# One more weight slot, one more raw tile, a longer lead of the first block, and later modulation sums in a two-layer decoder trunk

## The chip, the core and the metric

The kernel runs on one core of a Trainium2 chip. The metric is the device time of one execution in microseconds. TensorE (PE) does the matmuls, VectorE (DVE) and ScalarE (ACT) the elementwise work, GpSimd (POOL) a few small operations and some loads; SyncE (SP) issues nearly all loads from HBM.

## The reference, cut to what matters

256 tokens of width 1024 go through two layers. Each layer has three sub-layers, each with a residual:

```
mod = silu(c) @ ada_w[l] + ada_b[l]            # 9 vectors of 1024: shift, scale, gate of 3 sub-layers
h = rms_norm(x)*(1+sc1) + sh1;  x += 0.5*g1*swiglu(h)       # w_in 1024x5632, w_out 2816x1024
h = rms_norm(x)*(1+sc2) + sh2;  x += g2*token_mix(h)        # w_in 1024x2884, w_out 1024x1024
h = rms_norm(x)*(1+sc3) + sh3;  x += 0.5*g3*swiglu(h)
out = rms_norm(x)                                            # after the last layer
```

`token_mix` is a causal gating of 128-token chunks beside attention over the 64 best keys of an indexer. All is float32. The modulation vectors cost one pass over 75 MB of `ada_w`; all weights together are about 250 MB.

## The kernel before, in words

**Split products.** A float32 product is made of three fast ones: each weight tile is split into a high part `whi` (ACT, L455) and a low part `wlo` (DVE, L456), as the activations are, and `mm3` (L489 to L491) adds high by high, high by low, low by high. A *unit* is one weight tile of 128x1024. A split of a unit is called a conversion below.

**Phases and blocks.** The six sub-layers are phases 0 to 5: f, m, f, f, m, f (f for the feed-forward, m for the mixing). The tokens are two blocks of 128, b0 and b1. A generator per block (`ffn_gen`, `mix_gen`, `project`) yields after each unit. An f phase has 66 units: 8 for each block by itself, 36 that take both blocks at once (`joint_gen`, 256 columns, L672 to L676), then the 22 of the output product (`project`). An m phase has 24 units and 8 of `project`.

**Order.** `both` advances b0 while it is at most `LAG` items ahead of b1, else b1: so b0 runs `LAG`+1 units ahead, and at the end of a phase b1 has that many units left by itself. Then the next phase begins with b0 alone. After each item `item_done` runs what was deferred by a count of items, and `pump` issues up to one conversion.

**Slots.** Converted weights live in `NB` slots. `ring` keeps the order: a conversion may be issued when the slot `NB` conversions back has been released, and b1's item releases it. So in a steady stretch one conversion follows each item of b1, and its ACT part waits until TensorE has ended that item. Raw loads have `NRAW` tiles.

**Ends of a phase.** `project` goes through its units with both halves of 512 columns per unit, except the last `TAIL` units: there the first half of the columns is finished over all `TAIL` units, then the second. After the first half DVE makes `update` (L539, L541), ACT the squares (L502); after the second half `update` again, then `after_sub`: the sum (L510), the power on POOL (L512), the scaling (L516) and, `TRL` = 5 items later, `tr`: TensorE transposes of the scaled block (L733), scale and shift out of PSUM (ACT L527, DVE L529), and the split (ACT L534, DVE L535). `hold` keeps `pump` still for the item in which `after_sub` runs and the next one, and, for b1, also after the first half.

**Modulation.** `weave` puts the 8 tiles of each modulation vector between the units of a phase, evenly from unit `F0` to `F1` (f phases; `FA0`, `FA1` in phase 0) or `MA0` to `MA1` (m phases). `pump` adds such a tile to the sum when it comes to it in the sequence: the first by ACT (L435), the other seven by DVE (L440), one 128x1024 operation each. Eight items after the last tile a shift or scale vector is summed over partitions by two sets of four transposes and reductions (L403), a gate vector by four matmuls with ones. `VA1` to `VB2` say how many vectors each phase takes: 5, 1, 4 in layer 0, then 5, 0 and the last one.

In an m phase `sgu_out` (L954, hook of unit 22 of b0) writes `u`, which TensorE transposes one unit later.

Of the kernel before, what the change touches and what calls it, by code (L numbers as in the profile page):

```python
# [20 lines left out]
KF = DFF // P  # L21
DEPTH = 2
EPS = 1e-6
NB = 10
LEADJ = 8
LAG = 6
NRAW = 7
HOLD = 3
TAIL = 3
VX = 188  # L30
ADA_D = 8
D_EVP = 0
# [4 lines left out]
D_SC = 12  # L37
EV_D = 1
TR_D = 3
MA0 = 8  # L40
MA1 = 30
NG = 4
GW = D // NG
# [11 lines left out]
VA1 = 5  # L55
VA2 = 1
VA3 = 4
VB1 = 5
VB2 = 0
F0 = 14  # L60
F1 = 62
ADA0_ACT = 1
COL_D = 2
YH = 1
# [33 lines left out]
def trunk(ctx, tc, x_in, c_in, pos_in, ada_w, ada_b, norm_ffn1, ffn1_w_in, ffn1_w_out,  # L98
          norm_mix, mix_w_in, sgu_w, sgu_b, mix_w_out, norm_ffn2, ffn2_w_in, ffn2_w_out,
          final_norm, out):  # L100
    nc = tc.nc
# [3 lines left out]
    small = ctx.enter_context(tc.tile_pool(name="small", bufs=2))  # L105
    rawp = ctx.enter_context(tc.tile_pool(name="rawp", bufs=NRAW))
    hlp = ctx.enter_context(tc.tile_pool(name="hlp", bufs=NB))
    aap = ctx.enter_context(tc.tile_pool(name="aap", bufs=2))
# [4 lines left out]
    def take():  # L113
        return banks.pop(0)

    def give(*ts):
        banks.extend(ts)
# [134 lines left out]
    def weave(us, ads, lo, hi):  # L252
        res, n = [], len(ads)
        tot = max(n // KD * (KD + GAP), 1)
        pos = [lo + (hi - lo) * (i // KD * (KD + GAP) + i % KD + GAP // 2) // tot for i in range(n)]
        ai = 0
        for i, e in enumerate(us):
            while ai < n and pos[ai] <= i:
                res.append(ads[ai])
                ai += 1  # L260
            res.append(e)
        res += ads[ai:]
        return res
# [11 lines left out]
    names = [(l, nm) for l in range(DEPTH) for nm in ("A1", "B1", "G1", "A2", "B2", "G2", "A3", "B3", "G3")][2:]  # L275
    cuts = [VA1, VA2, VA3, VB1, VB2, len(names)]
    for l in range(DEPTH):
# [6 lines left out]
        for q in range(3):  # L284
            vl.append(sum((vecs(a, [nm]) for a, nm in names[:cuts[3 * l + q]]), []))
            names = names[cuts[3 * l + q]:]
        w1 = weave(u1, vl[0], FA0 if l == 0 else F0, FA1 if l == 0 else F1)
        if l == 0:
# [9 lines left out]
        seq += w1  # L298
        seq += weave(u2, vl[1], MA0, MA1)
        seq += weave(u3, vl[2], F0, F1)  # L300
    hold = [0]
# [8 lines left out]
    def defer(n, fn):  # L310
        pend.append([n, fn])
# [15 lines left out]
    def dma_fill():  # L327
        while dp[0] < len(seq):
# [5 lines left out]
            else:  # L334
                if n_r[0] - n_rd[0] >= NRAW:
                    break
# [75 lines left out]
    def pump(quota=2, force=False):  # L412
# [3 lines left out]
        while sp[0] < len(seq) and quota > 0:  # L416
# [8 lines left out]
            if e["k"] == "w" and not force and len(W) - wcur[0] >= lead[0]:  # L425
                break
            if need and r >= NB and not ring[r - NB]:
                assert not force, (r, ring[r - NB:], wcur, [q[0] for q in pend])
                break
# [36 lines left out]
    wcur = [0, 0]  # L466
    lead = [NB]

    def next_w(b):
        while wcur[b] >= len(W):  # L470
            pump(1, force=True)
        e = W[wcur[b]]
        wcur[b] += 1
        kt, cols = e["kt"], e["cols"]
        n = kt * cols
        return (e["hi"][:, :n].rearrange("p (k c) -> p k c", k=kt),
                e["lo"][:, :n].rearrange("p (k c) -> p k c", k=kt), e["slot"])

    def release(b, w):
        if b == 1:  # L480
            ring[w[2]] = True
# [6 lines left out]
    def mm3(ps, ahi, alo, whi, wlo, first, last):  # L488
        T.matmul(ps, ahi, whi, start=first, stop=False)  # L489
        T.matmul(ps, ahi, wlo, start=False, stop=False)  # L490
        T.matmul(ps, alo, whi, start=False, stop=last)  # L491
# [6 lines left out]
    def square(b, sl, first):  # L498
        if first:
            ssq[b] = [small.tile([P, 4], F32, name="ss", tag="ss"), 0]  # L500
        ss, c = ssq[b]
        S.activation(xm[b][:, sl], x[b][:, sl], AF.Square, accum_out=ss[:, c:c + 1])  # L502
        ssq[b][1] += 1
        if ssq[b][1] == 3:
            V.tensor_tensor(ss[:, 0:1], ss[:, 0:1], ss[:, 1:2], op=ALU.add)
# [32 lines left out]
    def update(b, l, i, acc, sl):  # L538
        V.scalar_tensor_tensor(xm[b][:, sl], acc, 1.0 if i == 2 else 0.5, vec[(l, "G", i)][:, sl],  # L539
                               op0=ALU.mult, op1=ALU.mult)  # L540
        V.tensor_tensor(x[b][:, sl], x[b][:, sl], xm[b][:, sl], op=ALU.add)  # L541

    def final_scale(b, sl):
        V.scalar_tensor_tensor(x[b][:, sl], x[b][:, sl], D ** 0.5, fin_g[0][:, sl], op0=ALU.mult, op1=ALU.mult)
# [25 lines left out]
    def project(b, pi, n, operand, hook):  # L570
        _, l, i, _ = phases[pi]
        final = pi + 1 == len(phases)
        parts = PARTS if final and b == 1 else HALF
        bk = [take() for _ in parts]
        acc = [t[:, :sl.stop - sl.start] for t, sl in zip(bk, parts)]

        def part(k, w, h):
            ahi, alo = operand(k)
            mm3(acc[h], ahi, alo, w[0][:, 0, parts[h]], w[1][:, 0, parts[h]], k == 0, k == n - 1)
        for k in range(n - TAIL):  # L580
            w = next_w(b)
            release(b, w)
            for h in range(len(parts)):
                part(k, w, h)
            hook(k)
            yield
        ws = [next_w(b) for _ in range(TAIL)]
        for h, sl in enumerate(parts):
            for i_ in range(TAIL):
                part(n - TAIL + i_, ws[i_], h)  # L590
                if h + 1 == len(parts):
                    release(b, ws[i_])
                if i_ == 1 and h == 0:
                    hook(n - TAIL)
                    yield
            if h < 2:
                hook(n - TAIL + h + 1)
            update(b, l, i, acc[h], sl)
            give(bk[h])
            if h == 0 and SQ_D and not final:  # L600
                defer(SQ_D, lambda b=b, sl=sl: square(b, sl, True))
            else:
                square(b, sl, h == 0)
            if final and h + 1 == len(parts):
                final_scale(b, parts[0])
            if h + 1 == len(parts):
                after_sub(b, pi)
            elif b == 1:
                hold[0] = 1 << 20
            if h != 1 or len(parts) == 2:  # L610
                yield
# [557 lines left out]
    for pi, (kind, l, i, n) in enumerate(phases):  # L1169
        with ExitStack() as es:  # L1170
            env = {}
            cnt = [0, 0]
            gens = {}

            def item(b):
                if b not in gens:
                    gens[b] = (ffn_gen if kind == "f" else mix_gen)(b, pi, env)
                next(gens[b])
                cnt[b] += 1
                item_done()  # L1180
                hold[0] -= 1
                if pi == 0 and cnt[0] > 10:
                    next(rope_it, None)
                pump(PQ)

            if pi == 0:
                with tc.tile_pool(name="startp", bufs=NSRAW) as sp_:
                    startp[0] = sp_
                    start(item)
            env["pool"] = es.enter_context(tc.tile_pool(name=f"ph{pi}", bufs=2))  # L1190
            one = es.enter_context(tc.tile_pool(name=f"po{pi}", bufs=1))
            if kind == "f":
                env["aThi"] = one.tile([P, KF, 2, P], F32R, name="aThi")
                env["aTlo"] = one.tile([P, KF, 2, P], F32R, name="aTlo")
            else:
                env["kiT"] = one.tile([P, 2 * P], F32, name="kiT")
                env["kT"] = one.tile([P, 4, 2 * P], F32, name="kT")
                env["v"] = one.tile([P, 2, 512], F32, name="vS")
            def both(stop):
                while cnt[1] < stop:  # L1200
                    if cnt[0] < stop and cnt[0] - cnt[1] <= LAG:
                        item(0)
                        if pi == len(phases) - 1 and cnt[0] == n - 10:
                            fin_g[0] = vecp.tile([P, D], F32, name="vec", tag="vec")
                            nc.sync.dma_start(fin_g[0], bcast_row(final_norm, D))
                    else:
                        item(1)
            if kind == "f":
                both(n - KF)
                lead[0] = LEADJ  # L1210
                for q, _ in enumerate(joint_gen(env)):
                    item_done()
                    hold[0] -= 1
                    if pi == 0:
                        next(rope_it, None)
                        next(rope_it, None)
                    pump(2)
                    if i == 1 and q == 4:
                        sgu_prep(l, env)
                        sguT[l] = env["sgu_T"]  # L1220
                        defer(6, env["sgu_fin"])
                lead[0] = NB
            both(n)


# [27 lines left out]
```

## Time and profile before

| | before |
|---|---|
| median of three runs | 1020.39 us (1020.06 to 1020.56) |
| the profiled execution | 1017.07 us |
| its span, first to last instruction | 1015.3 us |
| TensorE busy in it | 983.5 us, 97% |
| VectorE busy | 775.9 us, 76% |
| ScalarE busy | 539.0 us, 53% |
| GpSimd busy | 19.8 us, 2% |
| HBM read | 251.27 MB, 249 GB/s over the span |
| mean granted clock of TensorE | 0.997 |

The span is what the trace covers; 1.8 us of the execution lie around it. A busy share is over the whole span. Matmuls overlap one another in the records and their ends are modelled, so the distance from one matmul's start to the next says how fast TensorE goes. "Idle before" in a row is the time in which the engine stood still before that instruction, with what ended it.

### The profile page before, as it was taken

The page shows a single profiled execution, that of the slowest core. Times are in us where ns is not written, and L with a number is a line of the kernel's source. Part 1 is how long each engine was busy: PE and PEld are TensorE (multiplying, and loading weights), DVE is VectorE, ACT ScalarE, POOL GpSimd, SP SyncE. Part 2 cuts the span into 40 slices and gives each one's busy share as a digit, 9 for nine tenths or more (in the row PEclk, how much of TensorE's full clock was granted, in tenths as well). Part 3 has the DMA queues.
Part 4 walks back from the last instruction along what each step waited for, and adds up shares of the span by engine and source line. Part 5 has one row for each costly group of instructions (what it writes and reads, how often), then busy time and mean ns, then how long its engine had stood idle before and what let it go on. Part 6 is the DMA issues. An engine that isn't in the chain of part 4 may idle for free.

```text
span 1015.3 us, 16506 instructions
## 1 busy us (share of the span) xinstructions
PE 983.5 (97%) x6352; PEld 871.8 (86%) x6352; DVE 775.9 (76%) x1095; ACT 539.0 (53%) x832; POOL 19.8 (2%) x39
## 2 busy tenths in 40 slices
PE   5999999998999999999999999999999999999997
PEld 3699998887778799998878999987778879999886
DVE  3898988877997888887679798885879787566554
ACT  5575454446576645543456555534667766445341
POOL 4000000000000000000000000000000000000000
PEclk9999999999999999999999999999999999999999
DMA  9989899867664598878758899896555547665631
GB/s 328 340 309 339 316 380 346 317 203 230 192 188 146 168 346 313 313 273 289 273 161 289 341 330 353 320 343 193 157 147 156 154 146 259 250 218 188 217 116 42
DMA packets 109775, 253.40 MB, mean 250 GB/s; under 512 B 8499, under 2 KB 26981, under 8 KB 109697
## 3 DMA queue, kind: packets, MB, share of 16 engines
q1 hardware_dynamic: 108864, 251.20, 71.9%
q8 instruction: 50, 0.82, 0.3%
q0 software_dynamic: 544, 0.63, 0.2%
q10 hardware_dynamic: 288, 0.52, 0.1%
q14 instruction: 29, 0.23, 0.1%
HBM read 251.27 MB, written 1.05 MB: 249 GB/s over the span
## 4 chain that ended last, share of the span: by engine, by line
PE 84%; DVE 9%; ACT 3%; issue 2%; POOL 1%; DMA 1%; SPq 0%; POOLq 0%; ACTq 0%; DVEq 0%
PE bank L489 13%; PE bank L672 13%; PE bank L674 13%; PE bank L676 13%; PE bank L491 13%; PE bank L490 13%; PE bank L733 3%; DVE wlo L456 2%; DVE x L541 1%; ACT whi L455 1%; DVE xm L539 1%; PE bank L1047 1%; POOL rstd L512 1%; DVE aacc L1053 1%; DMA x<-in_x_dram 1%
## 5 line engine op out<-in xcount | busy, mean ns | idle before, releaser
L456 DVE TENSOR_TENSOR wlo<-raw,whi 128x1024 fp32r<-128x1024 f32 (+1 forms) x328 | 392.4, 1212 | 111.7 <-ACT whi L455 110.9
L455 ACT ACTIVATE whi<-raw 128x1024 fp32r<-128x1024 f32 (+1 forms) x328 | 334.4, 1045 | 217.4 <-PE bank L491 136.3
L672 PE MATMUL bank<-hThi,whi 128*128 128x256 f32 x1152 | 321.0, 279 | 0.0
L674 PE MATMUL bank<-hTlo,whi 128*128 128x256 f32 x1152 | 319.6, 277 | 0.0
L676 PE MATMUL bank<-hThi,wlo 128*128 128x256 f32 x1152 | 319.6, 277 | 0.0
L676 PEld LDWEIGHTS bank<-hThi,wlo 128*128 128x128 f32 x1152 | 217.6, 189 | 0.0
L672 PEld LDWEIGHTS bank<-hThi,whi 128*128 128x128 f32 x1152 | 216.3, 188 | 0.3
L674 PEld LDWEIGHTS bank<-hTlo,whi 128*128 128x128 f32 x1152 | 216.3, 188 | 0.3
L489 PE MATMUL bank<-whi,hThi 128*128 128x512 f32 (+1 forms) x384 | 154.5, 402 | 1.8 <-ACT hThi L1083 1.8
L491 PE MATMUL bank<-whi,hTlo 128*128 128x512 f32 (+1 forms) x384 | 149.0, 388 | 1.9 <-DVE hTlo L486 1.3
L490 PE MATMUL bank<-wlo,hThi 128*128 128x512 f32 (+1 forms) x384 | 147.6, 384 | 0.0
L440 DVE SCALAR_TENSOR_TENSOR aacc<-raw,ccol,aacc 128x1024 f32<-128x1024 f32 x112 | 143.1, 1278 | 0.0
L489 PE MATMUL bank<-whi,aThi 128*128 128x512 f32 (+1 forms) x374 | 142.3, 381 | 0.0
L490 PE MATMUL bank<-wlo,aThi 128*128 128x512 f32 (+1 forms) x374 | 141.2, 377 | 0.0
L491 PE MATMUL bank<-whi,aTlo 128*128 128x512 f32 (+1 forms) x374 | 141.0, 377 | 0.0
L489 PEld LDWEIGHTS bank<-whi,hThi 128*128 128x128 f32 x384 | 72.3, 188 | 19.8 <-issue 3.2
L491 PEld LDWEIGHTS bank<-whi,hTlo 128*128 128x128 f32 x384 | 72.1, 188 | 19.4 <-DVE hTlo L486 3.0
L490 PEld LDWEIGHTS bank<-wlo,hThi 128*128 128x128 f32 x384 | 72.3, 188 | 13.2 <-issue 0.5
L491 PEld LDWEIGHTS bank<-whi,aTlo 128*128 128x128 f32 x374 | 70.3, 188 | 13.3
L489 PEld LDWEIGHTS bank<-whi,aThi 128*128 128x128 f32 x374 | 70.4, 188 | 12.7
L490 PEld LDWEIGHTS bank<-wlo,aThi 128*128 128x128 f32 x374 | 70.4, 188 | 12.4
L681 ACT ACTIVATE xm<-bank 128x256 f32<-128x256 f32 x72 | 25.4, 379 | 62.5 <-PE bank L676 62.5
(150 smaller groups left out, 675.3 us busy)
## 6 DMA issues: line engine op xcount, KB each, us to landing
raw<-in_ffn_w_in_dram SPq DMA_DIRECT2D x176, 512.0 KB, 5.2
raw<-in_ada_w_dram SPq DMA_DIRECT2D x128, 512.0 KB, 5.7
raw<-in_ffn_w_out_dram SPq DMA_DIRECT2D x88, 512.0 KB, 5.3
raw<-in_mix_w_in_dram SPq DMA_DIRECT2D x40, 512.0 KB, 3.9
sraw<-in_ada_w_dram SPq DMA_DIRECT2D x32, 256.0 KB, 6.6
raw<-in_mix_w_out_dram SPq DMA_DIRECT2D x16, 512.0 KB, 3.6
vec<-in_ada_b_dram SPq DMA_DIRECT2D x6, 512.0 KB, 6.1
raw<-in_mix_w_in_dram SPq DMA_DIRECT2D x8, 324.0 KB, 3.0
```

The costliest lines, as they stand in the source:

```text
L440: V.scalar_tensor_tensor(aacc, e["raw"], ccol[:, j:j + 1], aacc, op0=ALU.mult, op1=ALU.add)
L455: S.activation(hi[:, :n], src, AF.Copy)
L456: V.tensor_tensor(lo[:, :n], src, hi[:, :n].bitcast(F32), op=ALU.subtract)
L489: T.matmul(ps, ahi, whi, start=first, stop=False)
L490: T.matmul(ps, ahi, wlo, start=False, stop=False)
L491: T.matmul(ps, alo, whi, start=False, stop=last)
L512: G.tensor_tensor(r, ms, mhalf, op=ALU.pow)
L672: T.matmul(o, wh[:, kk, sl], ahi, start=first, stop=False, skip_group_check=True)
L674: T.matmul(o, wh[:, kk, sl], alo, start=False, stop=False, skip_group_check=True)
L676: T.matmul(o, wl[:, kk, sl], ahi, start=False, stop=k == KD - 1, skip_group_check=True)
L681: S.activation(a, acc[j][:, :256], AF.Silu)
L733: T.transpose(ps[:, i * P:(i + 1) * P], src(i), ident)
```

## The change

The ring for loads that GpSimd issues is cut to 4096 bytes per partition (`dynamic_dma_scratch_size`), and the space goes to one more slot for converted weights (`NB` 10 to 11, a high and a low tile of 4 KB each) and one more raw tile (`NRAW` 7 to 8). In f phases b0 runs eight units ahead of b1 where it ran seven (`LAG` 7; in m phases it stays 6). The tail of `project` has two units where it had three, and the item that split the three-unit tail in two is gone; a project keeps the same number of items. Modulation tiles begin at unit 22 of an f phase in place of 14 and end at 64 in place of 62 (phase 0 keeps 20 and 66), and at unit 12 of an m phase in place of 8. The last shift vector of layer 1 moves from phase 3 to phase 4 (`VB1` 5 to 4, `VB2` 0 to 1).

```diff
-NB = 10
+NB = 11
-LAG = 6
-NRAW = 7
+LAG = {"f": 7, "m": 6}
+NRAW = 8
-TAIL = 3
+TAIL = 2
-MA0 = 8
+MA0 = 12
-VB1 = 5
-VB2 = 0
-F0 = 14
-F1 = 62
+VB1 = 4
+VB2 = 1
+F0 = 22
+F1 = 64
...
                 part(n - TAIL + i_, ws[i_], h)
                 if h + 1 == len(parts):
                     release(b, ws[i_])
-                if i_ == 1 and h == 0:
-                    hook(n - TAIL)
-                    yield
             if h < 2:
-                hook(n - TAIL + h + 1)
+                hook(n - TAIL + h)
...
-                    if cnt[0] < stop and cnt[0] - cnt[1] <= LAG:
+                    if cnt[0] < stop and cnt[0] - cnt[1] <= LAG[kind]:
...
-    nc = _bacc.Bacc("TRN2", target_bir_lowering=False, num_devices=1)
+    nc = _bacc.Bacc("TRN2", target_bir_lowering=False, num_devices=1,
+                     dynamic_dma_scratch_size=4096)
```

## Rows read from the trace of the kernel before

**Rows 1.** The page: span, and busy time of each engine.

```profile
span 1015.3 us, 16506 instructions
...
PE 983.5 (97%) x6352; PEld 871.8 (86%) x6352; DVE 775.9 (76%) x1095; ACT 539.0 (53%) x832; POOL 19.8 (2%) x39
```

**Rows 2.** Windows: stretch; length, busy of each engine, clock, DMA share, GB/s.

```profile
100.00:215.00 115.00, 115.00 (x761) 105.30 (x761) 97.49 (x108) 53.40 (x70) 0.00 (x0) 1.00 0.91 335
...
700.00:727.00 27.00, 24.15 (x114) 19.59 (x113) 20.22 (x32) 15.51 (x27) 1.10 (x2) 1.00 0.51 147
...
1000.00:1016.00 16.00, 8.20 (x53) 7.27 (x52) 6.60 (x16) 3.77 (x10) 1.46 (x2) 0.90 0.18 67
```

**Rows 3.** Waits of TensorE: total us, times, longest.

```profile
PE bank L733 <- DVE xm L516: 14.0, 8, 3.6
...
PE bank L733 <- DVE u L954: 1.5, 1, 1.5
PE bank L491 <- DVE hTlo L486: 1.3, 2, 0.7
```

**Rows 4.** Timeline of TensorE at phase ends and in the mixes: start, us.

```profile
232.69 1.09 PE L733 MATMUL bank<-ident,xm 128*128 128x128 f32 x8 [2.90 <-DVE xm L516]
...
294.20 0.66 PE L733 MATMUL bank<-ident,u 128*128 128x128 f32 x4 [1.53 <-DVE u L954]
...
531.91 1.09 PE L733 MATMUL bank<-ident,xm 128*128 128x128 f32 x8 [1.55 <-DVE xm L516]
...
709.16 0.39 PE L489 MATMUL bank<-whi,aThi 128*128 128x512 f32 x1
709.39 0.39 PE L490 MATMUL bank<-wlo,aThi 128*128 128x512 f32 x1
...
710.74 1.09 PE L733 MATMUL bank<-ident,xm 128*128 128x128 f32 x8 [0.74 <-DVE xm L516]
...
723.58 1.09 PE L733 MATMUL bank<-ident,xm 128*128 128x128 f32 x8 [2.11 <-DVE xm L516]
...
782.86 0.66 PE L733 MATMUL bank<-ident,u 128*128 128x128 f32 x4
```

**Rows 5.** Timeline of DVE at the end of phase 3.

```profile
705.91 1.23 DVE L456 TENSOR_TENSOR wlo<-raw,whi 128x1024 fp32r<-128x1024 f32 x1 [1.74 <-ACT whi L455]
...
716.28 2.36 DVE L456 TENSOR_TENSOR wlo<-raw,whi 128x1024 fp32r<-128x1024 f32 x2 [0.26 <-ACT whi L455]
718.56 0.68 DVE L539 SCALAR_TENSOR_TENSOR xm<-bank,vec 128x512 f32<-128x512 f32 x1
```

**Rows 6.** Timeline of DVE at the end of phase 2.

```profile
511.10 0.69 DVE L539 SCALAR_TENSOR_TENSOR xm<-bank,vec 128x512 f32<-128x512 f32 x1 [1.08 <-PE bank L491]
```

**Rows 7.** Timeline of DVE in the mixes of layer 0 and layer 1.

```profile
272.26 0.83 DVE L456 TENSOR_TENSOR wlo<-raw,whi 128x648 fp32r<-128x648 f32 x1 [0.96 <-ACT whi L455]
...
274.39 1.27 DVE L440 SCALAR_TENSOR_TENSOR aacc<-raw,ccol,aacc 128x1024 f32<-128x1024 f32 x1
275.58 0.48 DVE L819 SCALAR_TENSOR_TENSOR score<-rl,idx,negm 128x256 f32<-128x256 f32 x1
...
293.02 1.12 DVE L954 SCALAR_TENSOR_TENSOR u<-bank,sbT,u 128x128 f32<-128x128 f32 x4
...
763.08 0.83 DVE L456 TENSOR_TENSOR wlo<-raw,whi 128x648 fp32r<-128x648 f32 x1 [2.56 <-ACT whi L455]
...
781.69 1.12 DVE L954 SCALAR_TENSOR_TENSOR u<-bank,sbT,u 128x128 f32<-128x128 f32 x4
```

**Rows 8.** Timeline of DVE at the end of the kernel.

```profile
1006.09 0.69 DVE L539 SCALAR_TENSOR_TENSOR xm<-bank,vec 128x512 f32<-128x512 f32 x1 [3.73 <-PE bank L491]
...
1008.24 0.42 DVE L539 SCALAR_TENSOR_TENSOR xm<-bank,vec 128x256 f32<-128x256 f32 x1
```

**Rows 9.** Timelines of POOL and ACT: POOL's last idle, first use of POOL's loads.

```profile
217.18 0.57 POOL L512 TENSOR_TENSOR rstd<-ms,mhalf 128x1 f32<-128x1 f32 x1 [188.63 <-DVE ms L510]
...
88.66 0.60 ACT L745 ACTIVATE sguT<-bank 128x512 f32<-128x512 f32 x1 [3.56 <-PE bank L733]
```

## The prediction

> **What bounds the kernel now.** First the page: TensorE is busy 983.5 of 1015.3 us [rows 1]. Second the windows: in a middle stretch it has work in all of 115 us while loads run at 335 GB/s, and it stands still only at the start, at the kernel's end and around the ends of phases [rows 2]. Third the waits: apart from the start, TensorE waits for DVE alone, for the scaled block (L516), for `u` in the mix (L954) and for a low part (L486) [rows 3]. Fourth the timeline of TensorE: the scaled block is late by 2.90 us at the end of phase 0, by 1.55 at the end of phase 2, by 0.74 (b0) and 2.11 (b1) at the end of phase 3, and `u` by 1.53 in the mix of layer 0, by nothing in the mix of layer 1 [rows 4]. Between these places starts of 512-column matmuls stand 0.23 us apart [rows 4], so there is nothing else to win there. The change can thus act only through DVE's queue at phase ends, through DVE's queue in the two mixes, and at the very end. All these waits are 14.0 + 1.5 + 1.3 = 16.8 us, the start's with them [rows 3], so a gain of more than 1.6% is out of reach.
>
> **How a phase end works.** One item of a block is six matmuls, 6 x 0.23 = 1.38 us. From b0's scaling to b1's transposes DVE goes through one unbroken list: scaling, two conversions, shift and split of b0, two conversions, the two updates of b1, then the squares, power and scaling of b1. Two conversions take 718.56 - 716.28 = 2.28 us, so one is 1.14 [rows 5]. DVE ends this list after TensorE has run out of other work; the difference is the wait.
>
> **Longer lead and eleventh slot, f phases.** With eight items of b1 left in place of seven, TensorE gets 1.38 us more to do between b0's end and b1's transposes. But `pump` also runs once more before `hold` stops it: by the order in the code, conversions come after b1's second to fifth of seven items now, and after the second to sixth of eight then; the eleventh slot is what permits the fifth. It stands in DVE's list ahead of b1's updates. So the wait falls by 1.38 - 1.14 = 0.24 us for each of three ends, not by 1.38. Bounds: 1.38 if the fifth conversion is not in the list, 0 if DVE's list also takes a further small wait.
>
> **Tail of two.** For b0 at the end of phases 0, 3 and both mixes, `update` waits not for TensorE but behind a conversion whose ACT part waited for b1's item (1.74 us idle before wlo [rows 5]); the second half ends at the same time as before, 1.38 + 1.38 + 1.38 against 0.69 + 1.38 + 2.07 us after that item. Cost nothing. At the end of phase 2 `update` does wait for TensorE [rows 6]: a slot that a gate vector had used was free. There the list is counted from the end of b0's first half, and TensorE then has 2.07 - 1.38 = 0.69 us less to do before the second half ends. Cost 0.69 - 0.24 = +0.45 for that end. For b1 both halves end long before DVE comes to them: nothing.
>
> **End of phase 3.** The last vector there is now a scale vector whose last tile stands before unit 62. By the count of items its second set of four transposes falls between b0's first and second half, where TensorE otherwise goes on to wait; four such take about 0.45 us, an estimate (half of the 1.09 us of the eight at 723.58, less the modelled end of the last) [rows 4]. Its reductions fit into the 1.74 us idle [rows 5]. So -0.24 - 0.45 = -0.69 (bound: -0.24). Phase 0 keeps its places: -0.24. The three ends: -0.24 + 0.45 - 0.69 = **-0.48 us**.
>
> **Sums in the mix of layer 0.** With the eleventh slot a tile at position p is added after b0's unit p-5, where it was p-4. Positions 12, 14, 16, 18, 21, 23, 25, 27 give units 7 (ACT), 9, 11, 13, 16, 18, 20, 22; before, they were 8, 10, 13, 16, 19, 21, 24, 27, the middle ones at units 12, 15, 17, 20 and 23. DVE has no idle from 272.26 (b1's conversion of unit 16's pair) to `u` at 293.02 [rows 7]. Two sums lie in it before (after 17 and 20) and two then (18 and 20); the one after unit 16 fits into the 0.96 us idle ahead of 272.26 and what the moved sum leaves there. But the conversions are one unit further on, so one of the narrow ones (0.83 us, 648 columns) is a wide one (1.23 [rows 5, 7]): **+0.40**. Bounds: 0, and +1.6 if a third sum comes ahead of `u`.
>
> **Sums in the mix of layer 1.** Before, it has none, and `u` is just in time: TensorE starts the transposes with no idle [rows 4], within 0.1 us of DVE's end. The same list takes 293.02 - 272.26 = 20.76 us with two sums and 781.69 - 763.08 = 18.61 without [rows 7]; one sum is 275.58 - 274.39 = 1.19. So `u` comes 2.15 + 0.40 later, and with 0.05 of slack TensorE waits **+2.5 us**. Its transposes for that vector only move from phase 3. Bounds: 0 if the list has cover that I do not see, +3.7 with a third sum.
>
> **End of the kernel.** b1's last tail has pieces of 512, 256 and 256 columns. TensorE ends at the same time, but behind the first piece stand six matmuls of 256 columns less, at half of 0.23 us each, so it ends 0.69 us nearer to that end, and from its update at 1006.09, which waits for TensorE, DVE goes without a break to the last update at 1008.24 and the sum behind it [rows 8]. So the chain ends **+0.69** later; bounds 0 and 0.69.
>
> **Loads.** Later starts squeeze phase 2's 32 tiles into 42 units where they had 48: per unit 0.524 x (1 + 32/42) = 0.92 MB in 2.76 us, 334 GB/s, against 335 moved with TensorE never idle [rows 2]. Phase 3 has as many. One raw tile more only issues a load earlier on SP's queue, in the same order. Cost nothing; without that cover it would be a load's lateness, which no wait in the middle shows [rows 3].
>
> **The smaller ring of GpSimd.** GpSimd has no work between its start and 217.18, 188.63 us of idle, and what it loads last is first used at 88.66 [rows 9]; so a load that comes tens of us late is hidden. The Trainium skill (DMA: Bandwidth & Descriptors, SWDGE vs HWDGE vs iDMA) says that GpSimd itself writes the descriptors of its loads into rings in SBUF that the DMA engines drain, by which a ring of a quarter of the size could make GpSimd stand still; no run here shows such a wait, and by it the sum would still be the same up to some 60 us of standstill.
>
> **Sum.** -0.48 + 0.40 + 2.5 + 0.69 = +3.1 us. The profiled execution of 1017.07 (span 1015.3 and 1.8 around it) becomes 1020.2; it lies 3.3 below the median of the runs, and I carry the difference to the median: 1020.39 + 3.1 = **1023.5 us**.
>
> **Rivals.**
> 1. *The fifth conversion does not delay b1's update.* Then each f end gains 1.14 more: 1023.5 - 3.4 = 1020.1, no change. For it: `hold`, slots and loads might stop it. Against: in the trace two conversions stand right ahead of the update [rows 5], as the code's order says.
> 2. *The eleventh slot leaves one slot free, so that the conversion in b0's tail no longer waits for b1's item* (other side). That is the state at the end of phase 2, where the wait is 1.55 against 0.74 + 2.11 = 2.85 at the end of phase 3 [rows 4]: 1.3 us per end. It would act at four ends (phases 0, 1, 3, 4): 1023.5 - 5.2 = 1018.3, faster. It decides from the point where two of the four ends gain more than that and the mix costs less. Against: `pump` fills every slot that is released, so a further slot is filled too.
> 3. *A third sum comes ahead of `u`, or the low part of the gated output (behind the sum after unit 22) is late too*: 1.19 in each mix, 1025.9.
> 4. *The sums in layer 1 find cover*: 1023.5 - 2.5 = 1021.0, no change. Against: DVE's list there is as dense as in layer 0.
> 5. *GpSimd stands still for so long that TensorE waits*: unpriced by rows, each us beyond the cover one us.
>
> **Chances.** Forecast 0.44; rival 1 0.20, rival 2 0.23, rival 3 0.06, rival 4 0.06, rival 5 0.01. The measurement can tell 0.2%, 2 us, from no change: faster 0.23, same 0.27, slower 0.50. The range for 8 in 10 goes from rival 2's time to a little under rival 3's: 1018.2 to 1025.5; the forecast's own range is 1022 to 1025.
>
> **What would show it.** The wait of TensorE for `u` in layer 1 at 2 to 3 us, in layer 0 at about 1.9; between the two L456 pairs and L539 of b1 at f ends three conversions in place of two, and waits for L516 of about 2 us at phases 2 and 3; in the last 10 us the chain from L539 on shifted by 0.7. Wrong would be: no wait in the second mix, or `update` of b0 waiting for TensorE at the ends of phases 0 and 3.

## The result, and the profile after

The changed kernel is slower: 1024.08 us (median of 17 runs, 1021.22 to 1025.90) beside 1019.84 (17 runs, 1017.32 to 1020.80) for the kernel before; the plain medians differ by 4.2 us, but the runs lie on several chips, and the ratio of runs taken on the same chips is 1.0056, 95% interval 1.0044 to 1.0067. On the 1020.39 that the forecast started from, that ratio makes 1026.1, beyond the range's upper end of 1025.5. The direction is the forecast's; the loss is about 5.7 us where 3.1 was forecast.

The profiled execution of the changed kernel took 1023.01 us. The page of after, its first line and its line of engines:

```profile
span 1021.0 us, 16463 instructions
...
PE 986.2 (97%) x6352; PEld 873.4 (86%) x6352; DVE 774.6 (76%) x1095; ACT 537.3 (53%) x832; POOL 20.6 (2%) x39
```

The span is 5.7 us longer than before [rows 1], and TensorE is busy 2.7 us longer with the same 6352 matmuls. Waits alone would leave its busy time where it was, so a part of the loss is not waiting. The waits of TensorE after:

```profile
PE bank L730 <- DVE xm L516: 12.9, 7, 3.6
PE bank L1044 <- DMA sraw<-in_ada_w_dram: 5.1, 1, 5.1
PE bank L730 <- DVE u L951: 3.8, 2, 1.9
PE bank L491 <- DVE hTlo L486: 2.4, 2, 1.2
```

(Lines behind the removed ones are three lower than before: L733 is L730 now, L954 is L951. In e1 and e6 below, L733 is a matmul of the filler and L735 the transposes.) `u` is now late twice, 3.8 us in all where it was late once by 1.5 [rows 3]. The timeline of TensorE after, at the places of [rows 4]; the bracket is how long it stood still:

```profile
231.29 1.09 PE L730 MATMUL bank<-ident,xm 128*128 128x128 f32 x8 [3.35 <-DVE xm L516]
...
293.11 0.66 PE L730 MATMUL bank<-ident,u 128*128 128x128 f32 x4 [1.92 <-DVE u L951]
...
532.07 1.09 PE L730 MATMUL bank<-ident,xm 128*128 128x128 f32 x8 [1.92 <-DVE xm L516]
...
709.35 1.09 PE L730 MATMUL bank<-ident,xm 128*128 128x128 f32 x8 [0.22 <-DVE xm L516]
...
723.32 1.09 PE L730 MATMUL bank<-ident,xm 128*128 128x128 f32 x8 [1.91 <-DVE xm L516]
...
786.75 0.66 PE L730 MATMUL bank<-ident,u 128*128 128x128 f32 x4 [1.92 <-DVE u L951]
...
834.80 1.09 PE L730 MATMUL bank<-ident,xm 128*128 128x128 f32 x8 [0.96 <-DVE xm L516]
```

The last line stands for b1's last transposes (end of phase 4); before, they were:

```profile
829.81 1.09 PE L733 MATMUL bank<-ident,xm 128*128 128x128 f32 x8 [0.94 <-DVE xm L516]
```

Set beside [rows 4], place by place:

| place | before | after | difference | forecast |
|---|---|---|---|---|
| end of phase 0 | 2.90, and 0.4 for a low part just ahead | 3.35 | +0.05 | -0.24 |
| `u`, layer 0 | 1.53 | 1.92 | +0.39 | +0.40 |
| end of phase 2 | 1.55 | 1.92 | +0.37 | +0.45 |
| end of phase 3 | 0.74 + 2.11 | 0.22 + 1.91 | -0.72 | -0.69 |
| `u`, layer 1 | none | 1.92 | +1.92 | +2.5 |
| from b1's last transposes to the end | 1015.3 - 829.81 = 185.49 | 1021.0 - 834.80 = 186.20 | +0.71 | +0.69 |
| sum | | | +2.7 | +3.1 |

One more wait grew, in both mixes: that for the low part of b1's gated output (`hTlo` of L486). In the mix of layer 1, before and after:

```profile
817.17 0.50 PE L491 MATMUL bank<-whi,hTlo 128*128 128x512 f32 x1 [0.65 <-DVE hTlo L486]
```

```profile
822.15 0.50 PE L491 MATMUL bank<-whi,hTlo 128*128 128x512 f32 x1 [1.19 <-DVE hTlo L486]
```

It is 1.18 to 1.20 us in every profile with a tail of two and 0.65 to 0.66 in every one with a tail of three. It costs nothing by itself and isn't in the table: e8 and e10 further on differ in the tail alone, and from the end of phase 3 to this matmul they take 812.33 - 718.44 = 93.89 us and 814.23 - 720.34 = 93.89. TensorE only comes there sooner.

So the waits came out as forecast, within 0.6 at each place, and they explain about half of the 5.7 us. The fifth conversion of the forecast is there too. VectorE after, at the end of phase 3, where [rows 5] has two conversions in this place:

```profile
714.89 3.50 DVE L456 TENSOR_TENSOR wlo<-raw,whi 128x1024 fp32r<-128x1024 f32 x3 [0.26 <-ACT whi L455]
718.30 0.68 DVE L539 SCALAR_TENSOR_TENSOR xm<-bank,vec 128x512 f32<-128x512 f32 x1
```

The other half of the loss is seen in the windows. After, with the granted clock as the last column but two:

```profile
290.00:300.00 10.00, 8.08 (x36) 5.72 (x35) 9.93 (x17) 4.23 (x7) 0.00 (x0) 0.83 0.71 211
531.00:541.00 10.00, 8.93 (x36) 7.33 (x37) 8.72 (x13) 6.72 (x11) 1.30 (x2) 0.83 0.51 153
...
722.00:732.00 10.00, 8.68 (x35) 7.15 (x36) 7.70 (x16) 6.75 (x14) 0.56 (x1) 0.83 0.44 122
```

The same windows of the kernel before:

```profile
290.00:300.00 10.00, 8.47 (x47) 6.11 (x46) 9.86 (x20) 4.63 (x9) 0.00 (x0) 1.00 0.66 202
531.00:541.00 10.00, 9.09 (x44) 7.64 (x45) 9.27 (x14) 7.51 (x12) 1.14 (x2) 1.00 0.51 153
722.00:732.00 10.00, 8.42 (x43) 7.08 (x44) 7.87 (x16) 7.06 (x15) 0.56 (x1) 1.00 0.42 122
```

Three times TensorE's granted clock is at half, 1.2 GHz in place of 2.4, for part of the window, and 8 to 11 fewer matmuls run in it. Each time it comes right behind a standstill of 1.9 us. In the timeline of TensorE after, behind the end of phase 2:

```profile
533.23 0.46 PE L490 MATMUL bank<-wlo,hThi 128*128 128x512 f32 x1
533.49 0.63 PE L491 MATMUL bank<-whi,hTlo 128*128 128x512 f32 x1
533.91 0.63 PE L489 MATMUL bank<-whi,hThi 128*128 128x512 f32 x1
534.34 0.63 PE L490 MATMUL bank<-wlo,hThi 128*128 128x512 f32 x1
...
536.47 0.56 PE L489 MATMUL bank<-whi,hThi 128*128 128x512 f32 x1
536.87 0.39 PE L490 MATMUL bank<-wlo,hThi 128*128 128x512 f32 x1
537.10 0.39 PE L491 MATMUL bank<-whi,hTlo 128*128 128x512 f32 x1
```

Starts stand 0.43 apart from 533.49 on and 0.23 again from 536.87. Eight matmuls take 3.38 us there where they would take 8 x 0.23 = 1.84: one such fall costs about 1.5 us. Three cost 4.6. (Laid beside the same matmuls of the kernel before, those of after come 1.55, 1.59 and 1.57 us later behind the three stretches, counted from the transposes.) Against them stands the start, where it was the kernel before whose clock fell in its profiled execution:

```profile
0.00:30.00 30.00, 18.78 (x61) 11.20 (x62) 14.43 (x28) 14.71 (x36) 11.35 (x25) 0.94 0.97 336
```

In the profile after, the clock is 1.00 in that window, and the end of phase 0 comes 232.69 - 231.29 = 1.40 us sooner although its wait is no shorter; 0.3 of it was there ahead of the fall. 2.7 + 4.6 - 1.4 = 5.9, and the spans differ by 5.7.

That is one execution of each kernel. Of the 17 executions after, the five with a mean granted clock of 0.992 to 0.994 took 1021.2 to 1023.0 us, the twelve with 0.990 took 1023.5 to 1025.9: how often the clock falls differs from execution to execution, and it is the larger part of their spread. Their mean is 0.991; 67 executions of the kernel before, taken beside the experiments, have 0.9944. The difference of 0.0034 over 1020 us is 3.5 us, an upper estimate of what the additional falls cost in the mean, and the loss less the waits is 5.7 - 2.7 = 3.0.

### The profile page after: what moved, and what is told of

Same layout as the page of the kernel before. It is cut to its first block, busy times and chain, and to the rows that moved or that the text cites. A ratio compares the mean times of both kernels' runs of the same rounds, so it can differ in the third digit from the quotient of the medians.

```text
span 1021.0 us, 16463 instructions
## 1 busy us (share of the span) xinstructions
PE 986.2 (97%) x6352; PEld 873.4 (86%) x6352; DVE 774.6 (76%) x1095; ACT 537.3 (53%) x832; POOL 20.6 (2%) x39
## 4 chain that ended last, share of the span: by engine, by line
PE 81%; DVE 11%; ACT 3%; issue 3%; DMA 1%; POOL 1%; SPq 0%; POOLq 0%; ACTq 0%; DVEq 0%
PE bank L671 13%; PE bank L669 13%; PE bank L673 13%; PE bank L489 13%; PE bank L491 12%; PE bank L490 12%; DVE wlo L456 3%; PE bank L730 3%; ACT whi L455 1%; DVE x L541 1%; DVE xm L539 1%; DVE score L825 1%; PE bank L1044 1%; DVE m L824 1%; POOL rstd L512 1%
```

## Experiments

Two theories. **The clock** (A in the expectations): waits cost their length, and behind many a standstill of about 1.9 us the clock falls for a stretch and costs 1.5 us more. **Waits alone** (B): the sum of the forecast holds, and the rest is something else in one of the parts. (The expectations count the same waits 0.16 to 0.17 us longer than the brackets here: 2.09 for 1.92, 1.46 for 1.29. Differences between two experiments are differences of their ratios to the kernel before on the same chip; most have an uncertainty of about 1.6 us.)

**e1: TensorE kept at work ahead of the late transposes.** The changed kernel with 16 matmuls of constants into the bank that the transposes use.

```diff
+FILL_X = {(0, 2): 16, (1, 1): 16, (1, 2): 16}
+FILL_U = (16, 16)
...
+        for _ in range(fill):
+            T.matmul(ps[:, :P], ones, ones, start=True, stop=True)
```

> The changed kernel with 16 matmuls of ones by ones (128 columns) ahead of the transposes for which TensorE waits: those of u in both mixes, and those of b1's scaled block at the ends of phases 0, 2 and 3. Their result is written over. Theory A (a wait of some 2 us is followed by a stretch at half the clock, and that is what the forecast of +3.1 us left out): the granted clock stays at 1.00 in the stretches around 294, 533 and 724 us, where the changed kernel had 0.5 for some 3.4 us each; each fall cost about 1.5 us, so 3 to 5 us less than the changed kernel, 1018 to 1020 in the profile where it had 1023.0. Theory B (the falls are chance and the rest comes from loads or the start): the same time as the changed kernel within 1 us, and the clock still falls.

Ratio 1.0082 (1.0068 to 1.0096): by the ratios 2.7 us slower than the changed kernel, where A expected 3 to 5 less. The timeline of TensorE in e1, in the mix of layer 0 and at the end of phase 2:

```profile
293.86 2.25 PE L733 MATMUL bank<-ones 128*128 128x128 f32 x16 [1.93 <-DVE u L956]
295.90 1.07 PE L735 MATMUL bank<-ident,u 128*128 128x128 f32 x4
...
532.44 1.90 PE L733 MATMUL bank<-ones 128*128 128x128 f32 x16
534.52 1.09 PE L735 MATMUL bank<-ident,xm 128*128 128x128 f32 x8 [0.19 <-DVE xm L518]
```

At the ends of phases 2 and 3 the filler ran in place of the wait (at the end of phase 0 1.63 us of it were left), and the clock stayed at 1.00 behind phases 2 and 3. In the mixes it failed: the bank that the filler writes is the one that `u` reads and frees, so it stood behind the wait, put the transposes off by 2.0 us in the first mix and 2.6 in the second, and the clock fell behind both waits. As a whole the experiment decides nothing; its two halves point the same way.

**e2, e3, e4: parts undone, or one alone.** e2 is the changed kernel with one modulation vector back in phase 3; e3 is it with the tail of three and its code; e4 is the kernel before with the ring, the eleventh slot, the raw tile and the lead of seven and nothing else.

```diff
-VB1 = 4
-VB2 = 1
+VB1 = 5
+VB2 = 0
```

```diff
-TAIL = 2
+TAIL = 3
```

```diff
-NB = 10
+NB = 11
-LAG = 6
+LAG = {"f": 7, "m": 6}
-NRAW = 7
+NRAW = 8
...
```

(The item that splits the tail of three in e3, and the lines for the ring and for `LAG[kind]` in e4, are left out here.)

> The changed kernel with the last shift vector back in phase 3 (VB1 5, VB2 0). Theory of the forecast: TensorE's wait for u in the mix of layer 1 (2.09 us) is gone, the wait in layer 0 stays at 2.1; the end of phase 3 gets its 0.45 us of cover back or not by where the reductions fall: 2 us less than the changed kernel, up to 3.6 if a fall of the clock goes with the wait. Rival (the moved vector does not matter): no difference.

> The changed kernel with a tail of three units again. Theory of the forecast: the chain behind the last matmul is 0.69 us shorter and the wait at the end of phase 2 falls from 2.1 to 1.4, all other waits as in the changed kernel: 1.4 us less than the changed kernel. Rival (the tail is neutral, or two units free the slots earlier): no difference, or more time.

> The kernel before with the smaller ring, 11 slots, 8 raw tiles and eight units of lead in f phases, nothing else. Theory of the forecast: a fifth conversion takes back all but 0.24 us at each of three phase ends: 0.7 us less than the kernel before, not to be told from it. Rival 1 of the forecast (the conversion is off the path): 4 us less than before. Rival 2 (a slot stays free, so that the conversion in b0's tail does not wait): 5 us less, and the whi in b0's tail shows no wait for TensorE.

Measured: e2 1.0052 (1.0035 to 1.0070), e3 1.0015 (1.0004 to 1.0025), e4 0.9986 (0.9976 to 0.9995). In e2 the second wait for `u` is gone, but TensorE waits 1.0 us for a sum in phase 3, and b0's wait at its end is 0.72 again where the changed kernel has 0.22; it is no different from the changed kernel, where 2 us less was expected. From e4 to e3 the sums cost 2.9 us (forecast 0.40 + 2.5 - 0.45 = 2.45). From e3 to the changed kernel the tail of two costs 0.0041 x 1019 = 4.2 us, 2.6 to 5.8 by the intervals, where the forecast had 0.69 + 0.69 = 1.4. That is the term that failed. The timeline of TensorE in e3 at the end of phase 2:

```profile
531.33 1.09 PE L733 MATMUL bank<-ident,xm 128*128 128x128 f32 x8 [1.33 <-DVE xm L516]
```

The window of e3 there:

```profile
531.00:541.00 10.00, 9.67 (x47) 8.10 (x48) 9.04 (x14) 7.20 (x12) 1.44 (x2) 1.00 0.58 176
```

The timeline of TensorE in e4 at the ends of phases 0, 2 and 3:

```profile
231.53 0.77 PE L733 MATMUL bank<-ident,xm 128*128 128x128 f32 x4 [3.34 <-DVE xm L516]
...
530.83 1.09 PE L733 MATMUL bank<-ident,xm 128*128 128x128 f32 x8 [1.29 <-DVE xm L516]
...
722.27 1.09 PE L733 MATMUL bank<-ident,xm 128*128 128x128 f32 x8 [1.90 <-DVE xm L516]
```

As a wait the tail costs what was forecast: 1.92 - 1.33 = 0.59 here, and from b1's last transposes to the end e3 takes 1019.3 - 833.84 = 185.46, 0.7 less than after. But without it the clock stays at full behind this wait. In e4 the lead takes 1.55 - 1.29 = 0.26 and 2.11 - 1.90 = 0.21 from the waits of [rows 4] at the ends of phases 2 and 3, as forecast (0.24), not the 1.4 of the first rival; at the end of phase 0 it takes nothing.

**e5, e6, e7, e8: the clock, the tail, the conversions.** e5 is the changed kernel again, beside the others on one chip. e6 is e1 without the filler in the mixes. e7 is e4 with the tail of two (and without the item that splits the tail of three). e8 is e4 with conversions held for one item more behind a block's end.

```diff
-FILL_U = (16, 16)
+FILL_U = (0, 0)
```

```diff
-TAIL = 3
+TAIL = 2
```

```diff
-HOLD = 3
+HOLD = 4
```

> The changed kernel as it is, beside the three that follow, on one chip. Earlier the ratio to the kernel before was 1.0056. Theory A (each TensorE wait of about 2 us is followed in many executions by a stretch at half clock, worth some 1.5 us): 1.005 to 1.007 again, with stretches at half clock behind the wait for u in layer 0, behind the end of phase 2 and of phase 3. Theory B (the waits alone cost, as the forecast's sum has it): 1.0030.

> The changed kernel with 16 matmuls of constants ahead of b1's first transposes at the ends of phases 0, 2 and 3 (about 1.8 us of TensorE work that computes nothing, in place of standing still); the mixes are left alone. Theory A: no stretch at half clock behind the ends of phases 2 and 3, and 1.5 to 3 us less than the changed kernel of the same call, though no wait has become shorter. Theory B: the filler takes the place of the wait and nothing changes, or it costs up to 0.35 us per end.

> The small ring, the eleventh slot, the raw tile, the lead of seven and the tail of two; sums where they were in the kernel before. The lead alone ran at 0.9986. Theory B (the forecast's prices of the tail): +0.45 with +0.24 of it already counted, so 0.69 at the end of phase 2 and 0.69 at the kernel's end, 1.4 us above the lead alone: 1.0000. Theory A: the wait at the end of phase 2 grows from 1.46 to about 2.1 us, and a stretch at half clock follows it in part of the executions: 2 to 3 us above the lead alone, 1.0008 to 1.0016.

> The lead alone with conversions held back for four items behind a block's end in place of three. Theory of the forecast (each conversion in VectorE's list ahead of b1's updates takes 1.14 us of TensorE's wait): one conversion less at the ends of phases 0, 2 and 3, so waits of about 2.4, 0.3 and 0.9 us where the lead alone has 3.5, 1.46 and 2.06, and at most 1.1 less at the ends of phases 1 and 4: 3.4 to 5 us less than the lead alone, 0.994 to 0.995; with theory A another 1.5 to 3 us less, since the stretches at half clock behind the ends of phases 0 and 3 go too. Rival: the conversions that come later make the weights of the next items late, and the time stays within 1 us of the lead alone.

e5: 1.0062 (1.0042 to 1.0082), 1024.26 us. In its profile the clock fell behind the ends of phases 0, 2 and 3 and behind neither wait for `u`: the same kernel, other falls than in the first profile. e6: 1.0028 (1.0013 to 1.0042), 1020.23 us. Forty-eight matmuls that compute nothing make the changed kernel 4.0 us *faster* (3.5 by the ratios), more than A's 1.5 to 3. The timeline of TensorE in e6 at the end of phase 3:

```profile
719.41 1.90 PE L733 MATMUL bank<-ones 128*128 128x128 f32 x16
721.47 1.09 PE L735 MATMUL bank<-ident,xm 128*128 128x128 f32 x8 [0.17 <-DVE xm L518]
```

Its windows at the ends of phases 2 and 3:

```profile
531.00:541.00 10.00, 9.86 (x51) 8.26 (x50) 8.75 (x14) 7.43 (x12) 1.53 (x3) 1.00 0.55 162
721.00:731.00 10.00, 9.83 (x51) 8.15 (x51) 8.24 (x16) 7.07 (x14) 0.00 (x0) 1.00 0.52 155
```

The transposes start no sooner behind the last matmul that computes something (at the end of phase 3 721.47 - 719.18 = 2.29 us, in the changed kernel 723.32 - 721.02 = 2.30); only the standing still is gone, and the clock is 1.00. The mean granted clock over the executions is 0.9915 in e5 and 0.994 in e6. Waits alone can't give that: B falls.

e7: 1.0024 (1.0012 to 1.0037), 3.9 us above e4, 2.3 to 5.5 by the intervals: above the 2 to 3 that was expected of A, but not beyond the noise, and clear of B's 1.4. The timeline of TensorE in e7 at the end of phase 2:

```profile
532.82 1.09 PE L730 MATMUL bank<-ident,xm 128*128 128x128 f32 x8 [1.90 <-DVE xm L516]
```

Its window there:

```profile
532.00:542.00 10.00, 9.18 (x38) 7.54 (x39) 8.77 (x13) 6.46 (x11) 1.68 (x3) 0.83 0.52 162
```

The wait grew from 1.29 to 1.90, and there the clock fell. The waits that the tail adds to e4 and that cost time are 0.61 here and 0.7 at the kernel's end; the mean clock over the executions goes from 0.9944 to 0.9922, which over 1018 us is up to 2.2 us.

e8: 0.9958 (0.9942 to 0.9973), 1014.02 us, faster than both kernels. The timeline of TensorE in e8 at the ends of phases 0, 2 and 3:

```profile
229.72 1.09 PE L733 MATMUL bank<-ident,xm 128*128 128x128 f32 x8 [2.21 <-DVE xm L516]
...
527.63 1.09 PE L733 MATMUL bank<-ident,xm 128*128 128x128 f32 x8 [0.73 <-DVE xm L516]
...
718.44 1.09 PE L733 MATMUL bank<-ident,xm 128*128 128x128 f32 x8 [0.79 <-DVE xm L516]
```

One conversion less in VectorE's list takes 3.34 - 2.21 = 1.13 at phase 0 and 1.90 - 0.79 = 1.11 at phase 3 from the wait: the 1.14 of the forecast's working [rows 5] is right, and a conversion does stand in front of b1's updates. At phase 2 it takes 0.56 only; what holds the other half wasn't followed up. The profiled execution has no half-clock stretch between 200 and 1000 us, but it is one of the fastest of nine (mean clock 0.999; over the nine 0.996, in e4 0.994). By the ratios e8 is 2.8 us below e4, which is what the three waits lost; the 3.4 to 5 us, and A's 1.5 to 3 for the clock on top, were not seen in full.

**e9 to e12: the same edit on four kernels.** `HOLD` of four, as in e8, on the changed kernel (e9), on lead and tail (e10), and on the kernel before (e12); on the lead (e11) it is five:

```diff
-HOLD = 3
+HOLD = 5
```

> The changed kernel with conversions held back for four items in place of three. The same edit on the lead alone took 1.13, 0.57 and 1.11 us from the waits at the ends of phases 0, 2 and 3. If the conversions in VectorE's list are the whole of it: waits there of about 2.4, 1.5 and 0.95 us, 2.8 us less than the changed kernel, and with theory A (stretches at half clock behind waits of about 2 us and more) 3 us less still at the ends of phases 2 and 3: 1.0005 to 1.0015 against 1.0062. The waits for u stay at 2.09, so a stretch at half clock behind one or both of them stays in part of the executions. Theory B (waits alone): 1.0035.

> Lead and tail of two with conversions held for four items. On the plain lead the tail cost 3.9 us, where the waits that it adds (end of phase 2, kernel end) sum to 1.3. Theory A: here the wait at the end of phase 2 only grows from 0.89 to about 1.5, so no clock fall follows it and the tail costs its waits alone, 1.3 to 1.4 us above the lead with four: 0.9970 to 0.9975. Rival (the tail has a cost of its own that no wait shows): 3 to 4 us above it, 0.999.

> Lead alone with conversions held for five items: one conversion less still ahead of b1's updates. If the wait falls by 1.14 again wherever there is one: phase 0 from 2.37 to 1.2, phases 2 and 3 from 0.9 to about 0: 3 us less than with four, 0.993. Rival: conversions that come later make weights late behind the phase's start (with four, a wait of 0.2 us for a low part shows there already), and the time is that of four or worse.

> The kernel before with conversions held for four items: ten slots, seven raw tiles, lead of six. Two conversions stand in the list ahead of b1's updates there, one then. If 1.14 us of wait goes at each of the ends of phases 0, 2 and 3 as on the lead: waits of 1.9, 0.6 and 1.1, 2.9 us less than the kernel before: 0.997; the falls of the clock behind the ends of phases 0 and 3 go too, 1.5 us in part of the executions. Rival: with a lead of six there is less TensorE work to cover the late conversions, and a wait for a low part takes the gain back: 0.999 to 1.001.

e9: 0.9982 (0.9972 to 0.9992), by the ratios 7.5 us below the first measurement of the changed kernel and 8 below e5; the two waits at the ends of phases 2 and 3 fell to 0.79 and 0.78, which is 2.3 of them, phase 0 gave 1.1, and the rest fits the clock (mean over the executions 0.995 in place of 0.991, up to 4 us). It came out better than A's 1.0005 to 1.0015: in its profiled execution the clock didn't fall even behind the two waits for `u`. The second of them in the timeline of TensorE:

```profile
780.94 0.66 PE L730 MATMUL bank<-ident,u 128*128 128x128 f32 x4 [1.93 <-DVE u L951]
```

Its window:

```profile
780.00:790.00 10.00, 8.92 (x54) 6.90 (x56) 9.93 (x15) 5.79 (x14) 0.00 (x0) 1.00 0.63 183
```

So a wait of this length doesn't always bring the fall.

e10: 0.9968 (0.9956 to 0.9980), 1.0 us above e8, with an uncertainty of 2. The tail that costs 3.9 us on e4 costs about its waits alone where the wait at phase 2 is short; even the 0.6 at phase 2 isn't paid (0.74 beside 0.73 in e8), and the 0.6 at the kernel's end is what is left. A further cost of the tail, the rival's 3 to 4 us, isn't seen, though 3 is only just outside the noise.

e11: 1.0072 (1.0060 to 1.0084). Its waits of TensorE:

```profile
PE bank L490 <- DVE wlo L456: 4.3, 7, 0.8
PE bank L489 <- ACT whi L455: 4.0, 5, 1.9
```

With five, converted weights run out behind the phases' starts, 8.3 us of waits, of which e8 has 0.2: the rival came true. Of three, four and five on the lead, four is best. e12: 0.9970 (0.9958 to 0.9983): most of e8's gain doesn't need the lead of seven, which adds 1.2 us (the intervals overlap).

**All profiles together.** Between 200 and 1000 us the 14 profiles have 36 standstills of TensorE of 1.88 us and more; 20 of them are followed by a half-clock stretch. They have 28 of 1.18 to 1.63 us, and none of those is. Every half-clock stretch in that part of the profiles follows a standstill of the first kind. At the ends of phases 2 and 3 a standstill of 1.88 to 1.93 us is followed by one in 9 of 10 cases; with the filler in its place (e1, e6) in none of 4. But length alone doesn't decide: 17 of the 24 standstills of 1.88 to 1.94 us are followed by a stretch, none of the six of 2.1 to 2.9, and three of the six of 3.3.

The Trainium skill (TensorE: Matmul & The Clock Gate, HAM oscillation — how this bites in real kernels) describes a matmul kernel whose waits for loads, 3 to 5 us long, throw the clock back each time, so that the price is paid again at every wait. These traces agree in part: here waits of 1.9 us were enough, at 1.5 us of price, but not at every wait.

## Why the prediction was right in direction and too small

- **Which waits move, and by how much: right.** Ends of phases 2 and 3, `u` in layer 0 and the kernel's end came within 0.1 us, `u` in layer 1 within 0.6: VectorE's list there grew by the 2.55 us of the forecast (785.58 - 764.41 = 21.17 against 18.61), but had more cover than the 0.05 that was assumed. Phase 0 gained nothing; the wait for a low part ahead of it went into the longer one.
- **The fifth conversion: right.** The lead's extra item is eaten by it; e4 shows 0.2 at two of the three ends and nothing at phase 0, and e8 shows what one conversion weighs. So the first rival falls; the second too, since b0's wait at the end of phase 3 is the same in e4 (0.74).
- **Third and fourth rival: wrong.** Two sums lie ahead of `u` in each mix, as forecast, and `u` of layer 1 is late. The low part of the gated output, the third rival's other half, does come later, but by the tail and not by a sum, and without a cost.
- **Loads and the small ring: right.** TensorE's only wait for a transfer is the start's, 5.1 us as before; no load of GpSimd's is waited for later.
- **The step that failed: the sum.** It added each wait at its own length, with TensorE as fast behind a wait as before it ("so there is nothing else to win there"): a term for the clock stood at nothing, without a reason. Two of the lengthened waits (`u` of layer 0 from 1.53 to 1.92, the end of phase 2 from 1.55 to 1.92) and the new one came to the length behind which TensorE's clock often falls, and each fall is 1.5 us on top; the end of phase 3 had a wait of that length already. In the terms: the tail was priced at 1.4 and measured 4.2 and 3.9, of which its waits are 1.3; the sums 2.45 against 2.9 and the lead -0.7 against -1.4 are within the noise. Neither the range nor a rival held the clock. The trace of the kernel before gave little warning: its clock is 1.00 from 200 to 1000 us, behind waits of 2.90 and 2.11 too. What pointed to it were the 0.94 of its first 30 us and the 3.3 us by which that execution lay below the median, which the prediction carried over without asking what they were.

What stays open: what makes the clock fall behind 20 such waits and not behind the other 16, and so how often it falls in a kernel; profiles of single executions don't show that. Phase 0's wait of 3.3 us was followed by a fall in e4, e5 and e7, and by none in the changed kernel's first profile, e2 and e3. Where the falls of the executions without a profile lie is not shown either; only their mean clock is.

## What to carry to other kernels

Where TensorE is the bound, don't price a wait by its length alone: look at the granted clock behind waits like it, and price the fall too. A change that makes two waits a little longer can cost three times their sum (the tail: 1.3 us of waits, 4.2 and 3.9 measured), and one that shortens them can earn it back (e9). Count what stands on the other engine's list between two dependent pieces, and take a piece out of there (here one conversion, 1.1 us at two of three places and 0.56 at the third) before touching sizes, buffers or tails.

## What was not expected of the hardware

Filling a wait with matmuls of constants made a kernel faster by 4.0 us (1024.26 to 1020.23), since 1.9 us of standing still costs TensorE up to 1.5 us afterwards, at 0.43 us for a matmul of 512 columns in place of 0.23.
